# Raw weights loaded ahead of their split, the residual loaded by quarters with the first down operands on POOL's queue, and state-space units started by a table of steps

## The chip, the cores and the metric

The kernel runs on one core of a Trainium2 chip. The metric is the time of one execution on the device in microseconds (us), the median of several runs. One execution of each kernel is also profiled; all views of the trace are of that execution.

The engines, by the names the profile gives them: PE is TensorE (matrix products; its weight loads are PEld), DVE is VectorE, ACT is ScalarE, POOL is GpSimd, SP is SyncE, which in this kernel does nothing but start transfers. Each engine works through its own list of instructions in the order in which the program was laid out, and an instruction that waits holds up all that stand behind it on that engine.

## What is computed

One layer of a hybrid encoder over 2048 frames of 1024 features. A norm feeds one input projection. A quarter of its columns goes to a state-space layer (32 groups of 16 channels, each with 64 complex states), the rest to chunked attention (8 heads of 64, chunks of 64 frames, each looking at itself and the 8 chunks before). Both are normed and go through one output projection, then a SwiGLU block follows, both on the residual stream. Cut from the reference:

```python
h = rmsnorm(x, norm_mix_g)
proj = h @ w_in                       # u_ssm | q | k | v, 512 columns each
bu = einsum('bsgh,gph->bsgp', u, b_bar)
states = associative_scan(combine, (lam_bar, bu), axis=1)
y = einsum('bsgp,ghp->bsgh', states, c_mat).real + d_skip * u
y = gelu(y);  y = y * sigmoid(y @ w_glu + b_glu)
scores = einsum('bnqhd,bnkhd->bhnqk', qc, kb) / sqrt(64) + bias
out = einsum('bhnqk,bnkhd->bnqhd', softmax(masked scores), vb)
x = x + concat(rmsnorm(y), rmsnorm(out)) @ w_out
h2 = rmsnorm(x, norm_ffn_g)
x = x + (silu(h2 @ w_gate) * (h2 @ w_up)) @ w_down      # 2816 columns between
return rmsnorm(x, norm_final_g)
```

Everything is float32.

## The kernel before

**Numbers as two parts.** The matrix engine multiplies a shorter float format (`fp32r`), so each float32 operand is split in a high part, a cast on ScalarE, and a low part, a subtraction on VectorE (`split`, lines 153 to 156). A product is three matmuls, hi x hi, lo x hi and hi x lo (`mm3`, line 79). So before a matmul can start with a new weight tile its raw numbers must have landed, ACT must have cast them and DVE subtracted; rows with `hi`/`lo`, `w`, `c`, `hd` at line 156 are such splits.

**Stages, in us from the start of the span.** Until about 130: projection to the state-space input `u` and the first rows of attention. 130 to about 705: attention, into which the projections to q, k and v and the state-space units are woven. To 978: the state-space output's gate and the output projection. 980 to 1830: gate and up, as products of blocks with seven instead of eight block products (Strassen's way; B11, T1, T2, B22, T3, B21 and T4 name the seven). 1830 to the end: the down projection, again by seven, and the last norm.

**Attention.** There are 128 attention steps, four blocks of rows `sb` of 32 steps each, one step being one pair of heads of one group of chunks. A step computes scores `sc`, adds the bias (DVE, line 849), takes exponentials (ACT, line 852), transposes the probabilities `pt` (PE, line 82) and splits them into `pth` (ACT, line 867) and `ptl` (DVE, line 868). Between the steps stand pieces of *units*. A unit is a generator that yields after each piece; `Unit(gen, n, s0, s1, pre)` spreads its n pieces evenly over steps s0 to s1 - 1 and lets its first piece, the loads, run `pre` steps earlier. There are these units:

- `hT_unit`: loads and splits the 512 rows of the next block.
- `qk_unit(sb, pr)`: projects q and k of one pair of heads. Its first piece is `load_w` for two weight tiles. In block 0 these come from the input as `raw` tiles (line 689, two buffers) and are split into `w`; the split tiles are kept in memory as `wss` (`keep_w`, line 700) and later blocks load them from there (line 695). The matmuls into `pf` follow, then q and k are evacuated and split (`q2h`, `q2l`, `k`, lines 769 to 775).
- `v_unit(sb, fh)`: the same for v.
- `ssm_unit(b)`, for b = 0 to 7, four channel groups each. Loads of `U`, `Bst`, `Tm` and `Vm` (lines 564 on); after a pause of eight pieces the projection `X` in two pieces of two matmuls and four evacuations on ACT (line 588); then a scan over time on POOL alone (`step`, lines 602 to 605, and `carry`, lines 613 and 614), whose last states are moved into `XG` by four transfers that POOL starts (line 636); after nine more pieces the result `Y`, matmuls of `Tm` on `U` and `Vm` on `XG` (they go through `pj`), evacuation (line 646) and eight transfers to memory. `X` and `Y` use one buffer, and `U` has one buffer, so the loads of a unit wait for the `Y` of the one before.

Unit b of the state-space layer runs from step 2 + 15 b to 2 + 15 (b + 1); `SW = 15` sets that. In attention the order within a step is fixed by the program text, and a scheduler with estimated times may move instructions that are independent on the same engine.

**Down.** `down_phase` holds the output of the SwiGLU, already combined into the seven operands and stored as `hq`, and the weights, combined in advance, as `wc`. An `operand` (line 1487) loads 768 KB into a tile `hd` from a ring of ten tiles (line 1493, on SP) and splits it. `group(hf, f0, ...)` does the seven products for one half of the frames `hf` and three blocks of features from f0, and adds each to `acc` (line 1513). Each product is 36 matmuls (four banks of PSUM, three feature blocks, three matmuls each). In the first group of each half `load_acc` also loads the residual, eight tiles of 128 x 1024, 512 KB each (line 1518), right behind the first pair of operands in the text. Before its first product the last results `g` of gate and up have to be multiplied (DVE, line 1432) and stored (`hs<-g`, line 1434, on SP).

Of the kernel before, what the change touches and what calls it, by code (L numbers as in the profile page):

```python
# [49 lines left out]
SW = 15  # L50
# [46 lines left out]
def f32(ap):  # L97
    return ap.bitcast(F32)
# [557 lines left out]
class Unit:  # L656


    def __init__(self, gen, n, s0, s1, pre=0, done=0, light=1):
        self.gen, self.n, self.s0, self.s1, self.pre, self.done = gen, n, s0, s1, pre, done  # L660
        self.room = lambda a, b: sum(light if s % 4 == LPH else 1 for s in range(a, b))

    def advance(self, s):

        if s < self.s0 - self.pre:
            return
        want = 1
        if s >= self.s0:
            want += math.ceil((self.n - 1) * self.room(self.s0, s + 1) / self.room(self.s0, self.s1) - 1e-9)
        if s >= self.s1 - 1:  # L670
            want = self.n + 1
        while self.done < want:
            self.done += 1
            if next(self.gen, self) is self:
                self.done = 1 << 30


def att_phase(k, ident, S, aw, x0, roots):

    tc, nc, io, pfs = k.tc, k.nc, k.io, k.pfs  # L680
    with ExitStack() as cx:
        hT, vts, qk, keep = {0: tuple(zip(*x0))}, {}, {}, {}

        def load_w(sb, n):

            w = k.t(aw, "w", [P, 2, 1024], F32R, bufs=WB)
            if sb == 0:
                raw = k.t(aw, "raw", [P, 1024], bufs=2)
                nc.sync.dma_start(raw[:], io["w_qk"][n] if n < 8 else io["w_v"][n - 8])
                for ins in split(k, w[:, 0], w[:, 1], raw[:]):  # L690
                    if n in (0, 4):
                        k.tc.keep_in_program_order(ins)
                keep[n] = w
            else:
                nc.sync.dma_start(f32(w[:]), S["ws"][n])
            return w[:, 0], w[:, 1]
# [35 lines left out]
        def qk_unit(sb, pr):  # L732
            ws = [load_w(sb, n) for n in (pr, 4 + pr)]
# [48 lines left out]
        def v_unit(sb, fh):  # L782
            ws = [load_w(sb, 8 + 2 * r + fh) for r in range(2)]
# [143 lines left out]
        for sb in range(NSB):  # L927
            g0 = sb * 32
            C = CUT if sb < NSB - 1 else CUTL
            if sb > 0:  # L930
                if DB:
# [3 lines left out]
            units += [ Unit(qk_unit(sb, 1), QK_N, g0 + C[2], g0 + C[3], 2, light=LIGHT),  # L935
                      Unit(qk_unit(sb, 2), QK_N, g0 + C[3], g0 + C[4], 2, light=LIGHT), Unit(v_unit(sb, 1), V_N, g0 + C[4], g0 + C[5], 2, light=LIGHT),
                      Unit(qk_unit(sb, 3), QK_N, g0 + C[5], g0 + C[6], 2, light=LIGHT)]
        for b in range(NG // GB):
            units.append(Unit(ssm_unit(k, sp, psum, S, b, k.ssm_eng), SSM_N, 2 + int(SW * b), 2 + int(SW * (b + 1)), light=SL))
# [535 lines left out]
def down_phase(k, S):  # L1475
    tc, nc, io = k.tc, k.nc, k.io
    V, te = nc.vector, k.te
    with ExitStack() as cx:
# [8 lines left out]
        def operand(src, early=False):  # L1487
# [4 lines left out]
            with tc.high_priority() if early else ExitStack():  # L1492
                nc.sync.dma_start(f32(lo), src.rearrange("g p c -> p g c"))
# [3 lines left out]
        def group(hf, f0, g, acc, early):  # L1497

            fs = slice(f0, f0 + g)
            x, y = [bank(dx) for _ in range(4)], None  # L1500
            for n, on_x, first, r, c in ((B11, 1, 1, 0, 0), (T1, 0, 1, 1, 1), (T2, 1, 0, 0, 1), (B22, 0, 0, 0, 1), (T3, 1, 0, 1, 1), (B21, 0, 1, 0, 0), (T4, 1, 0, 1, 0)):
# [13 lines left out]
        def load_acc(hf, acc):  # L1515
            for i in range(KT):
                a = k.t((a0, a1)[hf], f"acc{i}", [P, HALF])
                nc.sync.dma_start(a[:], S["x1"][i * P : (i + 1) * P, hf * HALF : (hf + 1) * HALF])
                acc.append(a)
# [177 lines left out]
```

## Time and profile before

| | us |
|---|---|
| three runs | 2287.0, 2295.97, 2296.15; median 2295.97 |
| profiled execution | 2289.1 |
| its span, first to last instruction | 2287.1 |
| busy in the span: PE / DVE / ACT / POOL | 2171.6 / 1544.7 / 1000.6 / 348.7 |
| mean granted clock of TensorE | 0.978 of full |
| moved by transfers | 428.33 MB, of it 412.50 MB from hardware queues and 13.91 MB from the software queue, where POOL's transfers go |

The span is what lies between the first and the last instruction; 2.0 us of the execution lie around it. A row of the timeline has a start, a duration, the engine, the line, the operation, out<-in and shape, how many, and in brackets the idle time of that engine before it and what ended it. A group of waits has the total, the number and the longest. "SPq" rows are issues on SP; their duration includes the time the queue was held. The granted clock (PEclk) is the share of full speed that TensorE's throttle allowed.

### The profile page before, as it was taken

To read this page: it belongs to the slowest core of one execution; us is meant where nothing else is said; L and a number is where in the kernel's file an instruction comes from. 1 tells how busy PE (TensorE), PEld (TensorE's weight loads), DVE (VectorE), ACT (ScalarE), POOL (GpSimd) and SP (SyncE) were. 2 spreads that over 40 slices of the span, in tenths; PEclk is the share of its full clock that TensorE was granted. 3 is DMA by queue.
4 is the path that set the end of the run, shared out by engine and by line. 5 is a ranking of instruction groups with operands and counts; after the bars stand their busy time and mean duration, and the time that the engine had idled before them with its cause. 6 is when DMAs were issued, how large, how long until landed. Compare 5 with 4: busy or idle time off the path is not lost.

```text
span 2287.1 us, 30278 instructions
## 1 busy us (share of the span) xinstructions
PE 2171.6 (95%) x10632; PEld 1830.1 (80%) x10632; DVE 1544.7 (68%) x2695; ACT 1000.6 (44%) x1654; POOL 348.7 (15%) x813
## 2 busy tenths in 40 slices
PE   8988899999996899999999999999999989999997
PEld 6777688898985788878888887888888778888886
DVE  7755565555556766876776678666666477789776
ACT  6444555455557652343333335333333343344322
POOL 2245765455660000000000000000000000000000
PEclk9998999999998999999999999999999999999999
DMA  8767886666644534854465567555423297465552
GB/s 299 236 221 220 257 223 201 187 188 179 188 132 124 171 121 147 267 189 151 160 200 178 167 211 258 203 169 188 139 96 110 78 341 252 166 212 193 206 189 74
DMA packets 215256, 428.33 MB, mean 187 GB/s; under 512 B 38592, under 2 KB 61168, under 8 KB 208000
## 3 DMA queue, kind: packets, MB, share of 16 engines
q1 hardware_dynamic: 210368, 412.50, 55.3%
q0 software_dynamic: 4736, 13.91, 2.0%
q8 instruction: 83, 1.36, 0.2%
q14 instruction: 69, 0.57, 0.1%
HBM read 286.86 MB, written 129.00 MB: 182 GB/s over the span
## 4 chain that ended last, share of the span: by engine, by line
PE 80%; DVE 6%; DMA 4%; POOL 4%; issue 3%; ACT 1%; SPq 1%; DVEq 0%; POOLq 0%; ACTq 0%
PE X L79 20%; PE ps L79 19%; PE Y L79 10%; PE pf L79 9%; PE big L79 9%; PE W L79 5%; PE pj L79 4%; PE sc L79 2%; PE pt L82 2%; DMA xt<-in_xp 1%; DMA hd<-wc 1%; POOL X L605 1%; DVE lo L156 1%; POOL X L604 1%; POOL st L602 1%
## 5 line engine op out<-in xcount | busy, mean ns | idle before, releaser
L79 PE MATMUL X<-hi,c 128*128 128x512 f32 x1408 | 451.0, 391 | 6.9 <-DVE c L156 5.4
L79 PE MATMUL ps<-hd,hd 128*128 128x512 f32 (+1 forms) x1968 | 430.8, 381 | 6.1 <-ACT hd L156 4.5
L79 PEld LDWEIGHTS ps<-hd,hd 128*128 128x128 f32 x1968 | 358.0, 189 | 77.7 <-ACT hd L156 5.3
L79 PEld LDWEIGHTS X<-hi,c 128*128 128x128 f32 x1408 | 265.3, 189 | 63.4 <-DVE c L156 6.3
L79 PE MATMUL X<-lo,c 128*128 128x512 f32 x704 | 274.9, 391 | 0.0
L156 ACT CAST hd<-hd 128x1536 fp32r<-128x1536 f32 (+1 forms) x106 | 147.7, 1393 | 236.3 <-DMA hd<-hq 178.7
L79 PE MATMUL Y<-hi,c 128*128 128x512 f32 x704 | 224.7, 390 | 1.5 <-DVE u L1389 1.5
L156 DVE TENSOR_TENSOR hd<-hd 128x1536 fp32r<-128x1536 f32 (+1 forms) x106 | 174.4, 1646 | 29.1 <-ACT hd L156 28.4
L156 DVE TENSOR_TENSOR c<-S,c 128x512 fp32r<-128x512 f32 x176 | 121.0, 689 | 98.3 <-ACT c L156 98.0
L1385 ACT COPY u<-X 128x512 f32<-128x512 f32 x132 | 77.4, 587 | 200.7 <-PE X L79 200.7
L1513 DVE TENSOR_TENSOR acc<-acc,ps 128x512 f32<-128x512 f32 x196 | 130.9, 684 | 50.3 <-PE ps L79 47.8
L156 ACT CAST c<-S 128x512 fp32r<-128x512 f32 x176 | 109.4, 622 | 120.1 <-PE Y L79 61.6
L79 PE MATMUL pf<-hi,w 128*128 128x512 f32 x416 | 153.9, 422 | 8.4 <-ACT w L156 4.7
L79 PE MATMUL big<-m,woh 128*128 128x512 f32 x512 | 161.2, 396 | 0.0
L79 PEld LDWEIGHTS Y<-hi,c 128*128 128x128 f32 x704 | 132.5, 188 | 29.9 <-DVE u L1389 2.2
L79 PEld LDWEIGHTS X<-lo,c 128*128 128x128 f32 x704 | 132.8, 189 | 27.5
L156 ACT CAST c<-raw 128x512 fp32r<-128x512 f32 x132 | 82.3, 623 | 150.5 <-PE Y L79 68.5
L79 PE MATMUL Y<-lo,c 128*128 128x512 f32 x352 | 137.2, 390 | 0.0
L868 DVE TENSOR_TENSOR ptl<-pt,pth 128x640 fp32r<-128x640 f32 (+3 forms) x152 | 98.3, 647 | 47.5 <-ACT pth L867 45.9
L852 ACT ACTIVATE s<-s,mn 128x640 f32<-128x640 f32 (+4 forms) x128 | 98.0, 765 | 65.6 <-DVE mn L849 61.1
L867 ACT CAST pth<-pt 128x640 fp32r<-128x640 f32 (+3 forms) x152 | 83.8, 551 | 95.6 <-PE pt L82 91.5
L79 PE MATMUL W<-hi,c 128*128 128x512 f32 x352 | 115.5, 389 | 0.0
(441 smaller groups left out, 4169.9 us busy)
## 6 DMA issues: line engine op xcount, KB each, us to landing
w<-wss SPq DMA_DIRECT2D x36, 1024.0 KB, 6.0
hq<-g SPq DMA_DIRECT2D x140, 256.0 KB, 2.1
hd<-hq SPq DMA_DIRECT2D x42, 768.0 KB, 4.5
hd<-wc SPq DMA_DIRECT2D x42, 768.0 KB, 6.0
raw<-in_w_gate SPq DMA_DIRECT2D x44, 512.0 KB, 3.8
raw<-in_w_up SPq DMA_DIRECT2D x44, 512.0 KB, 4.3
wc<-px SPq DMA_DIRECT2D x66, 256.0 KB, 3.2
wss<-w SPq DMA_DIRECT2D x12, 1024.0 KB, 5.7
```

Source lines behind the costliest of these rows:

```text
L79: return self.tc.keep_in_program_order(self.tc.nc.tensor.matmul(*a, **b))
L82: return self.tc.keep_in_program_order(self.tc.nc.tensor.transpose(*a, **b))
L156: return nc.scalar.copy(hi, raw), nc.vector.tensor_tensor(lo, raw, f32(hi), op=ALU.subtract)
L602: eng.tensor_tensor(t[:, :, :, :n], src, ar, op=ALU.mult)
L604: eng.tensor_tensor(dst, dst, t[:, :, :, :n], op=ALU.add)
L605: eng.tensor_tensor(dst, dst, t2[:, :, :, :n], op=ALU.add)
L852: nc.scalar.activation(s[:, :nk], s[:, :nk], AF.Exp, bias=mn[:], scale=-1.0, accum_out=sums[sb, pr][:, hh, qp : qp + 1])
L867: nc.scalar.copy(pth[:, a:b, qp, :], pt[:, a:b, :])
L868: nc.vector.tensor_tensor(ptl[:, a:b, qp, :], pt[:, a:b, :], f32(pth[:, a:b, qp, :]), op=ALU.subtract)
L1385: nc.scalar.copy(u[:], ps[:])
L1513: V.tensor_tensor(a, a, ps[:], op=ALU.add)
```

## The change

Three things are edited.

1. `load_w` becomes `load_raw` and `load_ws`. In block 0 both raw tiles of a unit are loaded first, then, after a `yield`, both are split. The units of block 0 for qk(0,1), qk(0,2), v(0,1) and qk(0,3) get one piece more, `pre = 4` (the loads four steps ahead) and a new argument `mid = 2` (the second piece, the split, two steps ahead); both were two steps ahead. The first unit and v(0,0) keep load and split together. Later blocks load from `wss` as before.
2. `SW = 15` becomes the table `SU`: the eight state-space units start at steps 2, 19, 35, 49, 64, 78, 93 and 107 and the last ends at 122, instead of 2, 17, 32, 47, 62, 77, 92, 107 and 122.
3. In the down phase, in the first group of each half, the operands of a product are loaded in the text one product ahead; in the very first group (`early`) all fourteen operands are issued from POOL's queue (`aside`); and the residual is loaded in quarters, 128 x 512, 256 KB, four at a time in the order in which the products add to them.

```diff
-SW = 15
+SU = 2, 19, 35, 49, 64, 78, 93, 107, 122
@@ class Unit
-        want = 1
+        want = 1 if self.mid is None or s < self.s0 - self.mid else 2
         if s >= self.s0:
-            want += math.ceil((self.n - 1) * self.room(self.s0, s + 1) / self.room(self.s0, self.s1) - 1e-9)
+            want += math.ceil((self.n - want) * self.room(self.s0, s + 1) / self.room(self.s0, self.s1) - 1e-9)
@@ attention
-        def load_w(sb, n):
...
+        def load_raw(n):
+            raw = k.t(aw, "raw", [P, 1024], bufs=2)
+            nc.sync.dma_start(raw[:], io["w_qk"][n] if n < 8 else io["w_v"][n - 8])
+            return raw
+
+        def load_ws(sb, ns):
+            raws = [load_raw(n) for n in ns] if sb == 0 else []
+            if raws and ns not in ((0, 4), (8, 10)):
+                yield
+            ws = []
+            for i, n in enumerate(ns):
+                w = k.t(aw, "w", [P, 2, 1024], F32R, bufs=WB)
+                if raws:
+                    for ins in split(k, w[:, 0], w[:, 1], raws[i][:]):
+                        if n in (0, 4):
+                            k.tc.keep_in_program_order(ins)
+                    keep[n] = w
+                else:
+                    nc.sync.dma_start(f32(w[:]), S["ws"][n])
+                ws.append((w[:, 0], w[:, 1]))
+            return ws
...
-            ws = [load_w(sb, n) for n in (pr, 4 + pr)]
+            ws = yield from load_ws(sb, (pr, 4 + pr))
...
+            for gen, n, c in ((qk_unit(sb, 1), QK_N, 2), (qk_unit(sb, 2), QK_N, 3), (v_unit(sb, 1), V_N, 4), (qk_unit(sb, 3), QK_N, 5)):
+                units.append(Unit(gen, n, g0 + C[c], g0 + C[c + 1], 2, light=LIGHT) if sb else Unit(gen, n + 1, C[c], C[c + 1], 4, light=LIGHT, mid=2))
-            units.append(Unit(ssm_unit(k, sp, psum, S, b, k.ssm_eng), SSM_N, 2 + int(SW * b), 2 + int(SW * (b + 1)), light=SL))
+            units.append(Unit(ssm_unit(k, sp, psum, S, b, k.ssm_eng), SSM_N, SU[b], SU[b + 1], light=SL))
@@ down_phase
-                nc.sync.dma_start(f32(lo), src.rearrange("g p c -> p g c"))
+                (nc.gpsimd if aside else nc.sync).dma_start(f32(lo), src.rearrange("g p c -> p g c"))
...
-                h = operand(S["hq"][hf, fs, n], early and n in (B11, T1))
-                w = operand(S["wc"][fs, n], early and n in (B11, T1))
-                if n == B11 and f0 == 0:
-                    load_acc(hf, acc)
+            def load(m):
+                if m < len(order):
+                    n = order[m][0]
+                    soon = early and n in (B11, T1)
+                    ops[n] = operand(S["hq"][hf, fs, n], soon, early), operand(S["wc"][fs, n], soon, early)
+
+            if f0 == 0:
+                acc += [k.t((a0, a1)[hf], f"acc{i}", [P, HALF]) for i in range(KT)]
+                load(0)
+            seen = set()
+            for m, (n, on_x, first, r, c) in enumerate(order):
+                load(m + 1 if f0 == 0 else m)
+                if f0 == 0 and (r, c) not in seen:
+                    seen.add((r, c))
+                    load_acc(hf, acc, r, c)
+                h, w = ops.pop(n)
...
-        def load_acc(hf, acc):
-            for i in range(KT):
-                a = k.t((a0, a1)[hf], f"acc{i}", [P, HALF])
-                nc.sync.dma_start(a[:], S["x1"][i * P : (i + 1) * P, hf * HALF : (hf + 1) * HALF])
-                acc.append(a)
+        def load_acc(hf, acc, r, c):
+            for i in range(4 * r, 4 * r + 4):
+                cs = slice(hf * HALF + c * 512, hf * HALF + (c + 1) * 512)
+                nc.sync.dma_start(acc[i][:, c * 512 : (c + 1) * 512], S["x1"][i * P : (i + 1) * P, cs])
```

What this does to the order of instructions at three places, all in lists of one engine. Lines of the changed kernel are 8 to 21 higher than those of the kernel before.

VectorE about step 7 of attention, before. `w_1859` and `w_1864` are the weights of qk(0,2); `k_349` and `k_352` the keys of the pair of heads before; `ptl` and `yt` belong to the attention steps and to the evacuation of q and k.

```order
L892 TENSOR_TENSOR ya_1890<-pj_1891,yt_1900 64x512
L868 TENSOR_TENSOR ptl_1904<-pt_1905,pth_1903 128x128
L762 TENSOR_TENSOR yt_1915<-pf_1808,rsn_92 128x512
L849 ISA s_1944,mn_1945<-sc_1941,nbb_1549 128x512
L868 TENSOR_TENSOR ptl_1904<-pt_1948,pth_1903 128x128
L775 TENSOR_TENSOR k_349_1690<-yt_1915,k_349_1690 64x512
L775 TENSOR_TENSOR k_352_1693<-yt_1915,k_352_1693 64x512
L878 RECIPROCAL rs_2090<-sm_1566 128x8
L868 TENSOR_TENSOR ptl_1904<-pt_1948,pth_1903 128x128
L156 TENSOR_TENSOR w_1859<-raw_1860,w_1859 128x1024
L156 TENSOR_TENSOR w_1864<-raw_1865,w_1864 128x1024
```

And after, where the same weights are called `w_1856` and `w_1859` and the keys again `k_349` and `k_352`:

```order
L156 TENSOR_TENSOR w_1856<-raw_1780,w_1856 128x1024
L900 TENSOR_TENSOR ya_1884<-pj_1885,yt_1894 64x512
L156 TENSOR_TENSOR w_1859<-raw_1782,w_1859 128x1024
L876 TENSOR_TENSOR ptl_1898<-pt_1899,pth_1897 128x128
L770 TENSOR_TENSOR yt_1909<-pf_1812,rsn_92 128x512
L857 ISA s_1938,mn_1939<-sc_1935,nbb_1549 128x512
L857 ISA mn_1939 128x1
L876 TENSOR_TENSOR ptl_1898<-pt_1942,pth_1897 128x128
L783 TENSOR_TENSOR k_349_1690<-yt_1909,k_349_1690 64x512
L783 TENSOR_TENSOR k_352_1693<-yt_1909,k_352_1693 64x512
```

The two subtractions moved from behind the keys to ahead of them.

TensorE at the projection of state-space unit 0, whose two pieces are the matmuls into `pj_1816` and `pj_1823` (before):

```order
L79 MATMUL pf_1808<-hi_188_991,w_1607 128x512
L79 MATMUL pj_1816<-U_1705,Bst_1714 128x256 x2
L79 MATMUL pj_1823<-U_1705,Bst_1714 128x256 x2
L79 MATMUL sc_1830<-lo2x_1388,hi1x_1386 128x256
L79 MATMUL sc_1830<-lo2x_1388,lo1x_1387 128x256
L82 MATMUL pt_1837<-ident_79,s_1730 128x128 x4
```

And after, where they are `pj_1820` and `pj_1862`:

```order
L79 MATMUL pf_1812<-hi_188_991,w_1609 128x512
L79 MATMUL pj_1820<-U_1705,Bst_1714 128x256 x2
L79 MATMUL sc_1827<-lo2x_1388,hi1x_1386 128x256
L79 MATMUL sc_1827<-lo2x_1388,lo1x_1387 128x256
L82 MATMUL pt_1834<-ident_79,s_1730 128x128 x4
...
L79 MATMUL pf_1812<-hi_196_999,w_1609 128x512
L79 MATMUL pj_1862<-U_1705,Bst_1714 128x256 x2
```

The second piece of the projection moved behind the scores, the transposes and twelve matmuls of the q and k projection (18 rows in all); its evacuation on ACT splits four and four in the same way.

SP at the start of the down phase, before: four operands of B11 and T1, eight residual tiles, then the operands of T2.

```order
L1493 DMA hd_17187<-wc_76 128x3x512
...
L1518 DMA acc_3157_17127<-x_5_67 128x1024
L1518 DMA acc_3158_17129<-x_5_67 128x1024
...
L1518 DMA acc_3164_17141<-x_5_67 128x1024
L1493 DMA hd_17235<-hq_75 128x3x512
L1493 DMA hd_17239<-wc_76 128x3x512
```

After, the last rows of POOL's list are the fourteen operands (B11, T1, T2 and so on); SP's list has the residual of both halves instead:

```order
L1500 DMA hd_17127<-hq_75 128x3x512
L1500 DMA hd_17131<-wc_76 128x3x512
L1500 DMA hd_17135<-hq_75 128x3x512
L1500 DMA hd_17139<-wc_76 128x3x512
L1500 DMA hd_17187<-hq_75 128x3x512
L1500 DMA hd_17191<-wc_76 128x3x512
L1500 DMA hd_17243<-hq_75 128x3x512
```

```order
L1441 DMA hs_73<-g_16992 128x512
L1539 DMA acc_3156_17120<-x_5_67 128x512
...
L1539 DMA acc_3162_17126<-x_5_67 128x512
L1539 DMA acc_3283_18497<-x_5_67 128x512
L1539 DMA acc_3284_18498<-x_5_67 128x512
```

Sixteen quarters of the first half are followed on SP by the sixteen of the second (`acc_3283` and on), ahead of the operands of the second group. The order of TensorE's matmuls in the down phase is unchanged.

More of the change, by code (lines that the diff above doesn't have):

```diff
@@ L782, in v_unit @@
         def v_unit(sb, fh):
-            ws = [load_w(sb, 8 + 2 * r + fh) for r in range(2)]
+            ws = yield from load_ws(sb, (8 + fh, 10 + fh))
             yield
@@ L1499, in group @@
             fs = slice(f0, f0 + g)
+            order = (B11, 1, 1, 0, 0), (T1, 0, 1, 1, 1), (T2, 1, 0, 0, 1), (B22, 0, 0, 0, 1), (T3, 1, 0, 1, 1), (B21, 0, 1, 0, 0), (T4, 1, 0, 1, 0)
             x, y = [bank(dx) for _ in range(4)], None
[L1501 to L1505 removed]
+            ops = {}
+            def load(m):
[13 more added lines that the diff above has]
+                h, w = ops.pop(n)
                 if not on_x and first:
```

20 lines of the change are left out of this document (3 added, 17 removed).

## The prediction

> **What bounds the kernel now.** I read the page first. The chain of work that ended last is by four fifths matmuls of TensorE:
>
> ```profile
> PE 80%; DVE 6%; DMA 4%; POOL 4%; issue 3%; ACT 1%; SPq 1%; DVEq 0%; POOLq 0%; ACTq 0%
> ```
>
> The change takes no matmul away, so it can win only idle time of TensorE and the slow clock behind such idle time. Its idle time by cause is in the view of waits (total, times, longest); these groups the change can touch:
>
> ```profile
> PE pj L79 <- DMA Tm<-kts: 11.1, 4, 3.7
> PE pf L79 <- ACT w L156: 4.7, 1, 4.7
> PE ps L79 <- ACT hd L156: 4.5, 2, 2.7
> PE pj L79 <- DMA XG<-X: 3.6, 2, 1.9
> ```
>
> Together 23.9 us, 1% of the span. The timeline of TensorE shows where they stand (start, duration, instruction, then the idle time ahead of it and who ended it):
>
> ```profile
> 167.90 0.44 PE L82 MATMUL pt<-ident,s 128*128 128x128 f32 x2
> 173.01 0.79 PE L79 MATMUL pf<-hi,w 128*128 128x512 f32 x1 [4.67 <-ACT w L156]
> 177.42 0.31 PE L79 MATMUL sc<-k,q2h 128*128 128x128 f32 x1
> 193.50 0.87 PE L82 MATMUL pt<-ident,s 128*128 128x128 f32 x3 [3.36 <-DVE ptl L868]
> 212.53 0.67 PE L79 MATMUL pj<-XG,Vm 128*128 128x256 f32 x2 [1.68 <-DMA XG<-X]
> 281.66 0.67 PE L79 MATMUL pj<-XG,Vm 128*128 128x256 f32 x2 [1.94 <-DMA XG<-X]
> 300.02 1.35 PE L79 MATMUL pj<-U,Bst 128*128 128x256 f32 x5 [2.92 <-DMA Tm<-kts]
> 364.46 1.75 PE L79 MATMUL pj<-U,Bst 128*128 128x256 f32 x7 [3.00 <-DMA Tm<-kts]
> 1831.46 0.73 PE L79 MATMUL ps<-hd,hd 128*128 128x512 f32 x2 [1.78 <-ACT hd L156]
> 1833.25 16.16 PE L79 MATMUL ps<-hd,hd 128*128 128x512 f32 x70 [1.06 <-DVE hd L156]
> 1852.12 1.22 PE L79 MATMUL ps<-hd,hd 128*128 128x512 f32 x2 [2.70 <-ACT hd L156]
> ```
>
> A stall can cost more than its length. In two-microsecond windows (busy times, then the granted clock, the DMA share and GB/s):
>
> ```profile
> core 0: us, PE busy (x) PEld busy (x) DVE busy (x) ACT busy (x) POOL busy (x), PEclk, DMA share, GB/s
> 172.00:174.00 2.00, 0.99 (x2) 0.50 (x2) 1.01 (x1) 1.91 (x3) 1.92 (x4) 0.53 0.34 130
> 174.00:176.00 2.00, 1.96 (x5) 1.44 (x5) 1.67 (x2) 0.00 (x0) 1.92 (x2) 0.50 0.51 217
> 176.00:178.00 2.00, 2.00 (x8) 1.61 (x8) 0.02 (x1) 0.00 (x0) 1.84 (x5) 0.50 0.96 329
> 194.00:196.00 2.00, 2.00 (x7) 1.61 (x6) 0.72 (x2) 0.64 (x2) 1.69 (x5) 0.50 0.96 397
> 300.00:302.00 2.00, 1.98 (x10) 1.78 (x11) 0.00 (x0) 0.79 (x3) 0.00 (x0) 1.00 0.35 70
> 1854.00:1856.00 2.00, 2.00 (x5) 1.61 (x6) 1.76 (x1) 1.53 (x2) 0.00 (x0) 0.50 1.05 410
> ```
>
> After 4.67, 3.36 and 2.70 us of idling the clock stands at 0.50, after 2.92 at 1.00. Six microseconds at half clock do three of work: half of 0.99, 1.96 and 2.00 is 2.5 us from 172 to 178, so I charge 2.5 to 3 us for each such stall. The Trainium skill (TensorE: Matmul & The Clock Gate, HAM oscillation) says that idle gaps above about 3.4 us bring the slow clock; the 2.70 us gap shows that here a shorter one can, and by that rule the down phase would have 2.8 us less to win than I count.
>
> **Raw weights earlier.** Four units of the first 512 rows get their raw weights four steps ahead and split them two steps ahead. The first wait this meets is the one at 173.01. Around it stand on VectorE:
>
> ```profile
> 169.29 1.84 DVE L775 TENSOR_TENSOR k<-yt,k 64x512 fp32r<-64x512 f32 x2
> 172.99 2.68 DVE L156 TENSOR_TENSOR w<-raw,w 128x1024 fp32r<-128x1024 f32 x2 [1.47 <-ACT w L156]
> 188.77 1.23 DVE L156 TENSOR_TENSOR w<-raw,w 128x1024 fp32r<-128x1024 f32 x1
> 193.08 0.28 DVE L868 TENSOR_TENSOR ptl<-pt,pth 128x128 fp32r<-128x128 f32 x1
> ```
>
> The instructions are the same; two casts on ScalarE and two subtractions on VectorE (2.68 us) move ahead of the split of k. So k is late next: without the weights' wait TensorE would have nine matmuls (2.0 us at 16.16/70 = 0.23 each) from 168.35 to the scores now at 177.42, thus come at 170.4, but the k split, ending at 171.13 now, gets 2.68 us of VectorE ahead of it. Wholly exposed that makes 173.8, wholly in idle time 171.1; I take the middle, 172.4. Gain at that place 177.42 - 172.4 = 5.0, and 0.9 more as the half clock's rest behind it goes: 5.9 (4.5 to 7.2). At 193.50 the released row is `ptl` behind a second subtraction; the new order puts it ahead of that one and of a `ya` row, so some 2.0 of the 3.36 go, and with them the half clock: up to 5 more. The DMAs moved are two raw loads of 512 KB, on SP ahead of four q loads that nobody waits for in these views; I cost them at nothing.
>
> **Unit spacing.** But what stands next on the path is unit 0's scan. It runs so:
>
> ```profile
> 159.68 3.02 ACT L588 COPY X<-pj 64x256 f32<-64x256 f32 x8 [0.24 <-PE pj L79]
> 162.85 0.51 POOL L602 TENSOR_TENSOR st<-X,a 128x128 f32<-128x128 f32 x1 [24.00 <-ACT X L588]
> 205.53 1.21 POOL L636 DMA_DIRECT2D XG<-X x2 [0.30 <-POOL X L614]
> 304.31 0.50 POOL L602 TENSOR_TENSOR st<-X,a 128x128 f32<-128x128 f32 x1 [28.50 <-ACT X L588]
> 344.63 1.21 POOL L636 DMA_DIRECT2D XG<-X x2 [0.30 <-POOL X L614]
> DMA to landing us min/median/max: 2.4/4.6/7.9
> ```
>
> From eight evacuations to the last XG issued POOL takes 162.85 to 206.74, and TensorE waits for its landing until 212.53. In the new order the second half of unit 0's projection comes 18 matmuls (3.4 us) later and its evacuation is split four and four; half of the 3.02 us now overlaps, so the scan starts about 2 us later and XG lands at about 214.5. Against that, Y of unit 0 gets 5.7 us more work ahead of it (matmuls counted in the order, at 0.23 us for 512 columns). The old kernel has that work done at 212.5 + 5.7 = 218, so all that was won before is cut to 218 - 214.5 = 3.5. The wait for XG itself grows: 10.9 us won less these 3.5, plus the old 1.68, is 9 us, and a wait so long should bring half clock, 3 us again. Through unit 0: 0.5 won (bounds -2 if the scan starts the full 3.4 us later, 10.9 if it keeps up).
>
> The later units need three rows more, SP's issues (start, duration) and the first matmul of unit 2's Y:
>
> ```profile
> 285.58 3.61 SPq L649 DMA_DIRECT2D y<-X  x8
> 291.59 3.53 SPq L564 DMA_DIRECT2D U<-u  x7
> 348.70 0.59 PE L79 MATMUL pj<-U,Tm 128*128 128x256 f32 x2
> ```
>
> Unit 1 has 2.9 us more work between its projection and Y, so the 1.94 at 281.66 goes (+1.9). Unit 2's loads of U no longer stand behind a weight load on SP, which waited for its buffer and kept them from 289.19 to 291.59, 2.4 us; work before it is 0.5 less: +1.9 of the 2.92. Unit 3 gets 3.4 us more work between unit 2's Y and its own projection: the 3.00 go (+3.0). In exchange units 2 and 4 have 5.6 and 6.2 us less work under their scans. Unit 2's last XG is issued at 345.84, so with the shortest landing, 2.4, it is there 48.2 us after the projection began at 300.02. Y came at 348.70, 48.7 us after it, without a wait; with 5.6 less work it comes at 43.1: a new wait of up to 5.6 if the scan takes as long as now, 0 if it shrinks along. I take 4, near the upper end since the scan's instructions are unchanged, and 2 for half clock behind it (two chances in three of 3). For unit 4 I take 1.0 (0 to 2.2). Sum of the attention part: 0.5 + 1.9 + 1.9 + 3.0 - 6.0 - 1.0 = 0.3 won; from -7 to +15.
>
> **The down phase.** The rows that carry it (SP's rows are issues; the window's last columns are granted clock, DMA share, GB/s):
>
> ```profile
> 1831.56 5.88 SPq L1518 DMA_DIRECT2D acc<-x  x8
> 1837.58 0.44 SPq L1493 DMA_DIRECT2D hd<-hq  x1
> 1848.70 1.47 ACT L156 CAST hd<-hd 128x1536 fp32r<-128x1536 f32 x1 [12.84 <-DMA hd<-hq]
> 1842.00:1853.00 11.00, 8.30 (x35) 6.32 (x33) 5.91 (x7) 3.37 (x3) 0.00 (x0) 0.93 1.04 410
> ```
>
> Now eight residual loads (4.2 MB, 5.88 us of issue) stand ahead of T2's operands, which are issued at 1837.58, cast only at 1848.70, and TensorE waits 2.70 us for them at 1852.12. With the operands on POOL, idle by then, T2's pair goes out six microseconds sooner. This should take the 2.70 and the half clock behind it, 2.8: 5.5 won, nothing lost beside it while the queue delivers. Each POOL issue is charged 0.6 (1.21 for two, the XG row), off the path. The first wait, 1.78 and 1.06, I leave: the subtraction of the first weights still stands behind the last `g` product on VectorE; POOL's issue may be up to 1 us earlier or later. The extra sixteen small residual issues cost SP about another 5.9 us per half in a stretch where nothing that TensorE needs stands behind them until the second group, some 55 us on. I count the 5.5 in full; the bounds are -13 (rival 2 below) and 6.5 (the first wait a little shorter too).
>
> Sum: 0.3 + 5.5 = 5.8 us. The profiled execution took 2289.1 (span 2287.1 and 2.0 around it), which gives 2283.3. The three runs are 2287.0, 2295.97 and 2296.15, so their median stands 6.9 above the profiled one and would give 2290. I write 2283, the sum on the execution that it is made from.
>
> **Rivals.** (1) *The scan keeps up.* POOL's forty-four microseconds in unit 0 were partly slowed beside VectorE's subtractions; unit 2 takes 41.5 for the same work. If the moved splits no longer collide, XG comes two or three microseconds sooner, and if no wait exceeds the length that drops the clock, unit 0 keeps 6 to 7 instead of 0.5 and units 2 and 4 lose nothing: 5.8 + 6 + 7 = 18.8, or 2270. For it: the difference 43.9 against 41.5. Against: the order puts unit 0's second half later.
>
> (2) *Contention in the down phase, slower than before.* The new order puts all residual, 8.4 MB of both halves, on SP at once beside the operands on POOL; before, the second half came with the second group. From 1842 to 1853 the engines already run at a share of 1.04 and 410 GB/s. Residual and the pairs of T2, B22 and T3 (4.7 MB) are 13.1 MB, 32 us at 410 GB/s, where T3 is wanted within about 31 us of 1831 (16.16 us for two products, two more to come, less the splits). If POOL's queue gets half, a pair of 1.57 MB takes 7.7 us, less than a product's 8.2: no wait. If it gets a third, a pair takes 11.5 us, and three products wait 3.3 each with half clock behind them, 18.3 us against the 5.5 removed: with 0.3 from the attention part 2289.1 + 18.3 - 5.5 - 0.3 = 2302. It decides from a share of 0.47 down. The Trainium skill (DMA: Bandwidth & Descriptors, Queues, rings and completion order) says that each engine takes turns between the queues it has work for, packet by packet; by it the share would be about half, which is just on the good side. No run here shows both queues loaded.
>
> (3) *Units 2 and 4 wait at full price.* For it: their scans are the ones whose cover shrinks. Against: XG's landing has been as short as 2.4. Waits of 5.6 and 2.2 with 3 us of half clock after each cost 13.8 where I count 7: 2283.3 + 6.8 = 2290, no change.
>
> (4) *The down part does nothing:* POOL's T2 issue waits for buffers that TensorE and ScalarE still hold, so it goes out hardly before 1837. Then only 0.3 is won, 2289.
>
> **How the numbers follow.** The bound for faster and slower is 0.5%, 11.5 us, about what a measurement of this kernel tells from no change. Forecast 0.43, (1) 0.22, (2) 0.14, (3) 0.12, (4) 0.09. The forecast's own range is 2276 to 2291; it splits into 0.20 faster and 0.23 same, since it stands 5.8 below the profiled execution and 13 below the median. (1) is all faster. (2) gives 0.12 slower and 0.02 same, (3) 0.11 same and 0.01 slower, (4) 0.08 same and 0.01 slower. Sums: faster 0.42, same 0.44, slower 0.14. The range runs from just below rival 1 to rival 2, 2268 to 2302.
>
> **What would show it.** Right: no wait for `w` near 170; a wait for `XG` at unit 0 above 5 us with half clock; none at unit 1's; no `U` wait for units 2 and 3; in the down phase no gap before T2 and a clock of 1.00 from 1850 on. Wrong: the first XG wait under 3 us (rival 1), waits for `hd` after `DMA` at B22 or T3 (rival 2), or POOL's T2 issue later than 1836 (rival 4). The forecast fails as a whole if the state-space stage ends earlier or later than its waits account for, or if a new wait appears in gate and up, which the change leaves alone.

## The result and the profile after

| | before | after |
|---|---|---|
| median of 20 runs each, us | 2295.59 (2282.42 to 2302.85) | 2292.34 (2285.17 to 2300.38) |
| profiled execution, us | 2289.1 | 2293.41 |
| ratio | | 0.9992, 95% interval 0.9978 to 1.0005 |

No change that can be told. The forecast was 2283, 0.25% below the profiled execution of before. That the profiled execution got longer while the median got shorter lies within the spread of single runs, 20 us before and 15 us after; the verdict is the ratio, the trace tells where time moved.

The view of waits of the changed kernel, whole span, answers to the four groups of the prediction:

```profile
PE pj L79 <- DMA XG<-X: 14.2, 2, 8.4
PE pt L82 <- DVE ptl L876: 13.5, 11, 3.2
PE pj L79 <- DMA Tm<-kts: 8.1, 5, 3.8
PE ps L79 <- DVE hd L156: 2.0, 2, 1.8
PE ps L79 <- DVE acc L1534: 1.2, 1, 1.2
```

The wait for `w` is gone, that for `hd` went from 4.5 and 1.6 to 2.0, and that for `XG` grew from 3.6 to 14.2. TensorE's timeline of the changed kernel has the places:

```profile
171.23 0.44 PE L82 MATMUL pt<-ident,s 128*128 128x128 f32 x2 [3.20 <-DVE ptl L876]
218.44 1.19 PE L79 MATMUL pj<-XG,Vm 128*128 128x256 f32 x2 [8.45 <-DMA XG<-X]
235.53 1.10 PE L79 MATMUL pj<-U,Bst 128*128 128x256 f32 x4 [1.88 <-DMA Tm<-kts]
312.32 0.89 PE L79 MATMUL pj<-U,Bst 128*128 128x256 f32 x3 [0.66 <-DMA Tm<-kts]
376.40 0.89 PE L79 MATMUL pj<-U,Bst 128*128 128x256 f32 x3 [0.22 <-DMA Tm<-kts]
450.35 0.89 PE L79 MATMUL pj<-U,Bst 128*128 128x256 f32 x3 [1.59 <-DMA Tm<-kts]
499.64 0.77 PE L79 MATMUL pj<-XG,Vm 128*128 128x256 f32 x1 [5.79 <-DMA XG<-X]
633.02 0.68 PE L79 MATMUL pj<-XG,Vm 128*128 128x256 f32 x2 [1.95 <-issue]
722.16 0.79 PE L79 MATMUL pf<-gh,wgh 128*128 128x512 f32 x1 [6.81 <-ACT gh L156]
1842.33 57.00 PE L79 MATMUL ps<-hd,hd 128*128 128x512 f32 x250 [1.76 <-DVE hd L156]
1900.52 0.70 PE L79 MATMUL ps<-hd,hd 128*128 128x512 f32 x2 [1.19 <-DVE acc L1534]
```

The first matmul of the gate after attention, here at 722.16, stood in the kernel before at:

```profile
714.56 0.79 PE L79 MATMUL pf<-gh,wgh 128*128 128x512 f32 x1 [6.76 <-ACT gh L156]
```

So attention ends 7.6 us later. Since the matmuls other than the state-space ones come in the same order in both kernels, each can be set against its twin (times of the kernel before): the changed kernel is 6.8 us ahead at 207 us, 2.7 behind at 222 (after unit 0's Y), 0.1 behind at 485, 8.2 behind at 497 (after unit 4's Y), 4.8 behind ahead of unit 6's Y and 8.6 after it, 7.6 at the gate. By 1820 it is 9.9 behind (gate and up add 2.3, which is in no part that the change touches), by 1862 2.7, by 1903 4.2. The down phase gives 5.8 back; attention had lost more than that.

Two waits for XG are followed by the slow clock. Windows of the changed kernel (busy times, granted clock, DMA share, GB/s):

```profile
218.00:220.00 2.00, 1.56 (x4) 1.33 (x5) 0.00 (x0) 0.00 (x0) 0.00 (x0) 0.50 0.00 0
220.00:222.00 2.00, 2.00 (x7) 1.56 (x6) 0.00 (x0) 0.58 (x2) 0.00 (x0) 0.50 0.00 0
500.00:502.00 2.00, 2.00 (x6) 1.56 (x6) 0.00 (x0) 0.00 (x0) 0.00 (x0) 0.50 0.05 10
```

What unit 0 waited for stands on POOL:

```profile
166.18 0.53 POOL L602 TENSOR_TENSOR st<-X,a 128x128 f32<-128x128 f32 x1 [27.21 <-ACT X L588]
211.60 1.21 POOL L636 DMA_DIRECT2D XG<-X  x2 [0.30 <-POOL X L614]
492.15 1.21 POOL L636 DMA_DIRECT2D XG<-X  x2 [0.30 <-POOL X L614]
```

The scan starts 3.3 us later than before (166.18 against 162.85) and takes 46.6 instead of 43.9 us. In unit 4 the last issue starts at 492.8 and XG has landed at 500.1, 7.4 us later; in the kernel before the same unit's XG had landed 4.6 us after its issue, and Y came behind it. (All landing times here are counted from the start of the issue.) What XG met on its way were loads of the split weights, 1 MB each, on SP's queue:

```profile
209.73 0.72 SPq L702 DMA_DIRECT2D w<-wss  x1
490.17 0.33 SPq L702 DMA_DIRECT2D w<-wss  x1
560.07 0.32 SPq L702 DMA_DIRECT2D w<-wss  x1
624.94 0.33 SPq L702 DMA_DIRECT2D w<-wss  x1
```

The last two XG of units 0, 4, 5 and 6 were issued 0.1 to 2.6 us behind these and landed after 6.2 to 7.8 us. Unit 1's, beside loads of `xt`, took 7.2 and 7.8. Those of units 2, 3 and 7, with no large load beside them, landed after 2.4 to 5.0. The three units whose Y waits for XG (0, 4 and 6) are all among those with a weight load; units 1 and 5 had work enough ahead of their Y.

### The profile page after: what moved, and what is told of

It is laid out like the page before. It is cut to its first block, busy times and chain, and to the rows that moved or that the text cites. A ratio compares the mean times of both kernels' runs of the same rounds, so it can differ in the third digit from the quotient of the medians.

```text
span 2291.6 us, 30320 instructions
## 1 busy us (share of the span) xinstructions
PE 2172.1 (95%) x10632; PEld 1828.7 (80%) x10632; DVE 1542.1 (67%) x2695; ACT 1000.9 (44%) x1654; POOL 359.2 (16%) x827
## 4 chain that ended last, share of the span: by engine, by line
PE 73%; POOL 8%; issue 6%; DVE 4%; DMA 3%; ACT 2%; SPq 1%; DVEq 0%; POOLq 0%; ACTq 0%
PE X L79 20%; PE ps L79 17%; PE Y L79 10%; PE big L79 9%; PE pf L79 5%; PE W L79 5%; PE pj L79 3%; POOL X L605 2%; POOL st L602 1%; POOL st L603 1%; POOL X L604 1%; POOL X L614 1%; POOL fx L613 1%; PE sc L79 1%; PE pt L82 1%
## 5 line engine op out<-in xcount | busy, mean ns | idle before, releaser
L1500 POOL DMA_DIRECT2D hd<-hq x7 | 5.3, 764 | 1133.4 <-PE X L79 1121.1
L860 ACT ACTIVATE s<-s,mn 128x640 f32<-128x640 f32 (+4 forms) x128 | 98.0, 765 | 58.5 <-DVE mn L857 53.6
```

The lines of the kernel that those rows point to most:

```text
L860: nc.scalar.activation(s[:, :nk], s[:, :nk], AF.Exp, bias=mn[:], scale=-1.0, accum_out=sums[sb, pr][:, hh, qp : qp + 1])
```

## The experiments

Attention runs from the first score matmul to the first gate matmul. "Idle" adds up the gaps of TensorE above 0.2 us in it, in brackets those ahead of state-space matmuls; "slow clock" adds up what the clock record falls short of full speed. These three are from one profiled execution each, which can lie several us off the median. Before, e3, e7 and e11 have the same program text in attention and spread from 577.2 to 582.2, so 5 us in that column are no effect by themselves. The ratio is over several runs, in brackets its 95% interval.

| kernel | ratio to before | attention | idle | slow clock |
|---|---|---|---|---|
| before | | 582.2 | 57.5 (14.7) | 31.7 |
| the change | 0.9992 (0.9978 to 1.0005) | 589.6 | 64.0 (24.3) | 32.0 |
| e1 raw weights alone | 1.0013 (0.9998 to 1.0028) | 578.1 | 57.3 (16.6) | 27.9 |
| e2 spacing alone | 1.0015 (1.0 to 1.003) | 587.5 | 57.4 (19.3) | 34.3 |
| e3 down alone | 0.9968 (0.9956 to 0.9981) | 580.0 | 55.4 (12.4) | 31.8 |
| e4 without spacing | 0.998 (0.9966 to 0.9994) | 581.0 | 60.4 (18.1) | 25.8 |
| e5 raw, short scan | 1.0006 (0.9985 to 1.0027) | 578.6 | 57.9 (14.8) | 28.2 |
| e6 unit 4 longer | 1.0001 (0.9981 to 1.0021) | 589.9 | 66.1 (25.7) | 30.3 |
| e7 down, all on SP | 0.9974 (0.9957 to 0.999) | 577.2 | 56.5 (14.9) | 25.7 |
| e8 cover table | 0.9915 (0.989 to 0.994) | 566.1 | 47.5 (11.4) | 21.9 |
| e9 cover, no raw | 0.9915 (0.9887 to 0.9942) | 573.5 | 52.0 (13.1) | 25.7 |
| e10 cover, no pieces | 0.9947 (0.9929 to 0.9965) | 582.0 | 58.5 (19.3) | 29.9 |
| e11 down, whole residual | 0.9996 (0.9979 to 1.0013) | 578.6 | 57.1 (13.7) | 26.5 |
| e12 cover alone | 0.9961 (0.9939 to 0.9982) | 578.7 | 51.9 (15.3) | 31.6 |
| e13 cover, raw, down on SP | 0.9901 (0.9879 to 0.9924) | 564.6 | 45.0 (9.5) | 24.6 |
| e14 cover, no raw, down on SP | 0.9938 (0.992 to 0.9955) | 568.5 | 52.5 (12.8) | 19.7 |

**The three parts, one at a time and two together.** e1 to e3 are the kernel before with that part's hunks of the diff; e4 is the changed kernel with

```diff
-SU = 2, 19, 35, 49, 64, 78, 93, 107, 122
+SU = 2, 17, 32, 47, 62, 77, 92, 107, 122
```

> The kernel before with the raw weights ahead alone (spacing and down phase as before). Theory A (unit 0's scan on POOL is the bound behind the weights' wait): no wait for w at 173, TensorE comes to unit 0's Y some 10 us earlier and waits there for XG 8 to 12 us instead of 1.68, with half clock behind it; at 230 us it stands within 3 us of before, end of attention within 3 us, time ratio 0.999 to 1.002. Rival B (the moved splits themselves slow ScalarE, VectorE and POOL): later by 4 us or more at unit 0's Y, ratio above 1.002. Rival C (the gain is kept): ratio below 0.997.

> The kernel before with the table of steps alone. Theory A: the w wait of 4.67 stays; unit 0's XG wait near 0 to 4 (the scan starts 2 to 3 us later, 5.7 us more work ahead of Y); units 2 and 3 lose their load waits; units 4 and 6 wait for XG 4 to 6 and 1 to 2 us with half clock, as with the whole change; end of attention 2 to 8 us later than before, ratio 1.001 to 1.004. Rival B: spacing alone is harmless or a gain, ratio at or below 1.000.

> The kernel before with the changed down phase alone. All theories take it for the part that gains: attention as before, the T2 gap of 2.70 gone, 5 to 6 us gained from the first down product to the end, ratio 0.9970 to 0.9982. If it gains under 2 us, the gain seen in the whole change's profile came from the later start and not from the edit.

> The changed kernel with units every 15 steps again (raw weights ahead and down phase as changed). Theory A: attention as in the raw-alone run, down gain 5 to 6, together 3 to 7 us faster than before, ratio 0.997 to 0.9985, so better than the whole change by 2 to 6 us. Rival B: attention later than before by 4 us or more, ratio 0.999 to 1.001, no better than the whole change.

e4 came out within theory A's range, though its interval overlaps that of the whole change. The ratios add up: 1.0013, 1.0015 and 0.9968 make 0.9996, measured 0.9992. The down phase gains 0.3%, clearly; the two parts in attention give about as much back, each by itself not clear of nothing. In e1 the wait for `w` is gone and unit 0's Y is reached 8 us sooner, at 202 instead of 210, where TensorE stands until XG lands:

```profile
209.23 0.77 PE L79 MATMUL pj<-XG,Vm 128*128 128x256 f32 x1 [6.44 <-DMA XG<-X]
```

It goes on 3.3 us ahead of the 212.53 of before, and half clock and the next units' loads leave 1 us of that at 224. That is theory A, with a wait below what it said (6.44 against 8 to 12). It missed the end of attention, 4.0 us earlier than before where it had said within 3; the profile is of the fastest of e1's twelve runs, and the ratio shows no gain. In e2 the wait for `w` stays, so unit 0's Y does not wait at all, and units 1, 4 and 6 do, unit 4 with 4.55; the sign is what theory A said, the size near its lower end.

**Is it the scan?** e5 is e1 with

```diff
-    yield from carry(Xk[:, :, :, 1:, :7], Xk[:, :, :, : NC // 8 - 1, 7], 0, NC // 8 - 1)
+    if b:
+        yield from carry(Xk[:, :, :, 1:, :7], Xk[:, :, :, : NC // 8 - 1, 7], 0, NC // 8 - 1)
+    else:
+        yield
+        yield
```

> The kernel before with the raw weights ahead alone, and the last, longest carry of unit 0's scan (four pairs of POOL instructions of 128x434) left out, so that unit 0's state is not the reference's. Theory A (unit 0's scan is what swallowed the gain): XG of unit 0 lands about 8 us sooner than in the raw-alone run, the 6.44 us wait falls below 1, TensorE stands 6 to 8 us ahead of the kernel before at 223 us, and keeps 4 to 8 of it to the end unless unit 1's or 2's loads and scan take it again; ratio 0.996 to 0.999. Rival (the time is lost anyway, to the later units' loads and scans, which are spaced as before): the gain at 223 is there but under 2 us is left at 350 us; ratio 1.000 or above.

The ratio is the rival's, the reason neither's: the scan ends 9.5 us sooner and the wait hardly moves, 5.08 instead of 6.44. The timelines of e5 on POOL, SP and PE show it:

```profile
197.14 1.21 POOL L640 DMA_DIRECT2D XG<-X  x2 [0.30 <-POOL X L614]
...
193.88 1.06 SPq L712 DMA_DIRECT2D wss<-w  x2
194.99 2.61 SPq L690 DMA_DIRECT2D raw<-in_w_qk  x2
...
208.79 0.77 PE L79 MATMUL pj<-XG,Vm 128*128 128x256 f32 x1 [5.08 <-DMA nbb<-nbs]
```

The row of TensorE names `nbb`; of the four XG the third landed at 208.52, just ahead of it. The last XG is issued at 197.8 and has landed at 209.7, 12.0 us later; in e1 it took 2.5. Ahead of it in time SP had issued two kept weight tiles of 1 MB and two raw tiles of 512 KB, and the engines were full:

```profile
198.00:202.00 4.00, 3.62 (x30) 3.39 (x29) 2.26 (x9) 2.73 (x10) 0.35 (x1) 1.00 1.10 256
```

So right behind the scan stands a second bound at the same time, 209 us. That it is this traffic which holds XG up is argued from the rows; a run without it was not made. For it: the same two raw loads, issued at 194.01 and 195.18 in e1, where the first XG went out only at 200.95, landed there after 7.9 and 8.0 us, and here, beside all four XG, after 12.7 and 14.0. What follows is that a shorter scan alone isn't the cure; e8 tries more work ahead of Y.

**Which unit's cover.** e6 is the change with `SU = 2, 19, 35, 49, 64, 79, 93, 107, 122` (79 for 78).

> The changed kernel with one number of the table moved: unit 4 ends and unit 5 starts at step 79 instead of 78. Theory A (unit 4's cover decides): unit 4 gets 5.5 us more work under its scan, its XG wait of 5.79 falls below 1.5 without half clock, unit 5 has 3.6 us less and still does not wait more than 1; attention ends 6 to 10 us sooner than in the whole change, ratio to before 0.995 to 0.9975. Rival (XG lands late there because of what else is moved at that time): the wait stays above 3, ratio 0.9985 or above.

Its wait for XG at unit 4 is gone, as theory A said, but the time is not: unit 5, whose step was taken, waits for its loads and then for XG (and unit 0's wait came out 1.0 longer, 9.45).

```profile
515.43 1.19 PE L79 MATMUL pj<-U,Bst 128*128 128x256 f32 x2 [2.51 <-DMA Tm<-kts]
...
566.86 0.67 PE L79 MATMUL pj<-XG,Vm 128*128 128x256 f32 x2 [1.88 <-issue]
```

Theory A held for the mechanism and failed in the sum: one number can't be moved alone, since units share a fixed number of steps. e8 therefore sets all of them by the matmuls that stand under each scan (38 to 48 us), and gives unit 0 more without parting its projection; e10 is e8 without the pieces:

```diff
-SU = 2, 19, 35, 49, 64, 78, 93, 107, 122
+SU = 2, 19, 34, 49, 63, 78, 92, 107, 122
@@ ssm_unit
-    for _ in range(YX):
+    for _ in range(YX + 5 * (b == 0)):
@@ units
-            units.append(Unit(ssm_unit(k, sp, psum, S, b, k.ssm_eng), SSM_N, SU[b], SU[b + 1], light=SL))
+            units.append(Unit(ssm_unit(k, sp, psum, S, b, k.ssm_eng), SSM_N + 5 * (b == 0), SU[b], SU[b + 1], light=SL))
```

> The changed kernel with another table (2, 19, 34, 49, 63, 78, 92, 107, 122) and five more empty pieces ahead of unit 0's Y alone, so that unit 0's projection is not parted and its Y has 39 us of work ahead of it instead of 34, and each later unit 38 to 48. Theory A (cover under each scan decides): unit 0's XG wait falls from 6 to 8 us to 0 to 3, no other XG wait above 2; with the down gain of 7 attention gains 2 to 7, ratio 0.994 to 0.9965, the best of the kernels so far. Rival (the gain is eaten by load waits of the next units): ratio 0.9965 to 0.9985.

> The changed kernel with that table alone, without the five empty pieces, so that unit 0's projection is parted in two again and its Y has 36 us of work ahead instead of 39. Theory A (unit 0's scan starts too late for its Y): unit 0's XG wait is back at 6 to 9 us with half clock, attention 8 to 11 us longer than with the pieces, ratio 0.995 to 0.9965. Rival (the later units' spacing is what gained, and a late unit 0 is made up by them): ratio 0.991 to 0.9935.

e8 is 0.85% faster than before, more than expected, and unit 0's Y hardly waits. What is left is unit 5:

```profile
211.55 0.67 PE L79 MATMUL pj<-XG,Vm 128*128 128x256 f32 x2 [0.47 <-DMA XG<-X]
...
544.76 1.19 PE L79 MATMUL pj<-XG,Vm 128*128 128x256 f32 x2 [3.19 <-issue]
```

Without the five pieces (e10), the same row reads:

```profile
218.88 1.19 PE L79 MATMUL pj<-XG,Vm 128*128 128x256 f32 x2 [8.98 <-DMA XG<-X]
```

That is 8.5 us more of wait and, by ratios taken on different chips, 7 us of time (0.9947 against 0.9915; the intervals overlap a little). The parting of unit 0's projection, a by-product of the wider spacing, is the start of it and not the whole: TensorE comes 1.2 us earlier to this Y, the last two XG are issued 1.9 us later, and the first of them lands after 8.6 instead of 3.2 us. In e8 they go out ahead of the next 1 MB weight load, in e10 with it (e8's two rows first, then e10's):

```profile
208.12 1.21 POOL L636 DMA_DIRECT2D XG<-X  x2 [0.30 <-POOL X L614]
210.68 0.32 SPq L702 DMA_DIRECT2D w<-wss  x1
210.05 1.21 POOL L636 DMA_DIRECT2D XG<-X  x2 [0.30 <-POOL X L614]
210.09 0.55 SPq L702 DMA_DIRECT2D w<-wss  x1
```

Unit 5 shows the same without an edit: e8 and e13 (below) have the same program text in attention. In e8 the first of its last two XG is issued 0.1 us behind such a load, they land after 7.1 and 8.3 us, and Y waits 3.19. In e13 the first of them is issued 1.5 us ahead of it, and they land after 3.4 and 4.1, and Y, which came 1.4 us later there counted from the projection, does not wait. e12 against e9 and e14, again with one attention text, is the same: 6.7 and 8.0 us behind the load, 2.8 to 3.1 ahead of it. Over all the traces, 38 of the 40 last XG that were issued with such a load or up to 2.7 us behind it landed after 6.2 to 8.9 us (the two others, of unit 1 in e1 and e4, after 3.4 and 2.6). No run moved the weight loads alone.

**Are the weights worth moving?** e9 is e8 without the hunks of the raw weights. e12 is the kernel before with e8's table and pieces alone. e13 and e14 are e8 and e9 with all down operands on SP, on one chip.

> The table of the best kernel so far (2, 19, 34, 49, 63, 78, 92, 107, 122, five empty pieces ahead of unit 0's Y) and the changed down phase, but the weights loaded and split as before the change. Theory A (moving the raw weights pays once unit 0's Y has cover): the w wait of 4.7 with half clock is back and nothing makes it up, attention 4 to 9 us longer than with the weights ahead (566 us there), ratio 0.993 to 0.9955. Rival (the table alone does it, the weights ahead are worth nothing): attention within 3 us of 566, ratio below 0.9925.

> The kernel before with the other table (2, 19, 34, 49, 63, 78, 92, 107, 122) and the five empty pieces ahead of unit 0's Y, nothing else. Theory A (the spacing's effect has the sign of the cover that it leaves under each scan): attention 5 to 10 us shorter than before, ratio 0.9945 to 0.9975, where the change's own table alone gave 1.0015. Rival (any spacing other than 15 steps only pays together with the changed down phase or the weights): ratio 0.999 or above.

> That table and pieces, the raw weights ahead and the changed down phase with its operands on SP's queue. Theory A (the weights ahead pay once unit 0's Y has cover): 3 to 7 us less than the run without them in this call, ratio 0.990 to 0.993. Rival (worth nothing): within 2 us of it.

> The same without the raw weights ahead. Theory A: 3 to 7 us more than the run with them in this call, ratio 0.992 to 0.995, attention 4 to 9 us longer. Rival: within 2 us of it, attention within 3 us.

e9 against e8, measured on different chips, fits the rival by the ratio (0.9915 both) and theory A by the profile (7 us, but of the slowest of e9's six runs). On one chip e13 and e14 have medians of 2268.76 and 2278.25, 9.5 us apart, more than theory A's 3 to 7; their intervals just touch, and in the profiles attention is 3.9 us longer, just short of the 4 to 9 expected. The profiled execution of e14, 2271.24, is the fastest of its six. In it the old wait stands:

```profile
171.33 0.80 PE L79 MATMUL pf<-hi,w 128*128 128x512 f32 x1 [4.67 <-ACT w L156]
```

So the weights ahead are worth nothing without cover (e1), and probably something with it: 9.5 us by the medians of the one pair on one chip, nothing by the ratios of the other pair. How much stays open. e12 shows the sign of the spacing turn with e8's table and pieces alone: 0.9961, where the change's own table gave 1.0015 (attention is 3.5 us shorter in its profile, less than theory A said and within the spread of one program). e13, at 0.9901, has the lowest ratio of the versions tried and is faster than both kernels; e8's interval overlaps its own.

**The down phase.** e7 is e3 with all operands on SP; e11 is e7 with the residual whole again:

```diff
-                (nc.gpsimd if aside else nc.sync).dma_start(f32(lo), src.rearrange("g p c -> p g c"))
+                nc.sync.dma_start(f32(lo), src.rearrange("g p c -> p g c"))
@@ e11 also (its load_acc with whole tiles is not shown)
...
-                if f0 == 0 and (r, c) not in seen:
-                    seen.add((r, c))
-                    load_acc(hf, acc, r, c)
+                if f0 == 0 and m == 0:
+                    load_acc(hf, acc)
```

> The kernel before with the changed down phase alone, but all operands on SP's queue: one product ahead and residual by quarters are kept, POOL's queue is not used. Theory A (POOL's queue is what gets T2's operands out ahead of the residual): a wait for hd of 2 us or more with half clock at T2 or B22 is back, ratio 0.999 to 1.001. Rival (order of loads and quarters do it alone): no such wait, ratio as with POOL's queue, 0.996 to 0.998.

> The kernel before with the changed down phase on SP's queue, but the residual in eight whole tiles of 512 KB, all of them ahead of T2's operands again. Theory A (the order of the residual against T2's operands is what gained, and quarters are what allows it): a wait for hd of 2 to 4 us with half clock at T2 is back, ratio 0.999 to 1.001. Rival (it is the loads one product ahead): no such wait, ratio 0.9965 to 0.998.

The rival wins in e7: without POOL's queue the gain is the same (0.9974 against 0.9968). After the first two waits the row of e7 runs through 126 matmuls without a gap:

```profile
1828.10 0.73 PE L79 MATMUL ps<-hd,hd 128*128 128x512 f32 x2 [2.25 <-ACT hd L156]
1829.89 30.45 PE L79 MATMUL ps<-hd,hd 128*128 128x512 f32 x126 [1.06 <-DVE hd L156]
```

With the residual whole, and the operands still one product ahead in the text, T2's gap is back and the gain gone (0.9996), as theory A said:

```profile
1827.64 16.17 PE L79 MATMUL ps<-hd,hd 128*128 128x512 f32 x70 [1.12 <-DVE hd L156]
1846.89 1.01 PE L79 MATMUL ps<-hd,hd 128*128 128x512 f32 x2 [3.08 <-ACT hd L156]
```

It is the quarters that allow the order: with them one MB of residual instead of four stands ahead of T2's operands. Quarters without the loads one product ahead were not run, and the intervals of e7 and e11 overlap, so that the gap at T2 carries this reading.

## Why the prediction failed, step by step

The step that failed is the sum for attention, 0.3 won: it mis-sized the waits for XG at units 0 and 4 and left out the one at unit 6. The runs showed 7.6 us lost there in the profile. At units 4 and 6 XG landed late, behind weight loads that the sum did not count; at unit 0 the scan started later and took longer than summed.

- **What bounds it:** right. No matmul went, and time moved with waits and with the slow clock behind them.
- **Raw weights:** the wait for `w` went; what came late next was not k but `ptl` (3.20 at 171.23), which the two subtractions also stand ahead of. The wait at 193.50 did shrink, to 1.49 (at 188.32). TensorE was 6.8 us ahead before unit 0's Y, where 10.9 had been summed up.
- **Unit 0's scan:** the mechanism was right and said ahead: a wait of 9, measured 8.45, with half clock. Mis-sized was XG's landing, 214.5 against 218.4: the scan started 3.3 instead of 2 us later and took 2.7 us longer. The longer scan goes with the moved splits: it took 45.3 to 46.6 us in the seven kernels that have them (e5 aside) and 43.9 to 44.6 in the eight that do not. Instead of 0.5 won, 2.7 were lost through unit 0.
- **Waits of units 1 to 3:** about right. Unit 1's 1.94 for XG went; the load waits of 2.92 and 3.00 became 0.66 and 0.22. A new one of 1.59 came at unit 4.
- **Units 2, 4 and 6, the step that failed most.** Unit 2 was given a wait of 4 and has none: its scan took 38.1 instead of 40.9 us from the first `st` to the start of the last XG issue, and TensorE needed 4.1 us more for the work under it, 2.4 of idling and 1.7 of half clock, which the prediction had not counted, so that the missing wait was in part luck. (The sum there also adds 2.4 to the end of the last issue, 345.84, while the view counts landings from its start, 345.25; that XG landed at 348.73.) Unit 4 was given 1.0 and cost 8 with its half clock. Its bound of 2.2 comes out with XG's landing at 2.4, the shortest in the profile; here the last two landed after 7.4 us, behind the 1 MB weight load issued at 490.17. In the kernel before that load was issued at 490.02, when XG had landed (487.89). Unit 6's wait (1.95, and 3.9 with the clock) was not seen at all; its last two XG landed after 7.4 and 7.8 us, behind the load issued at 624.94. So the sum for attention was 0.3 won and came out as 7.6 lost in the profile; by the runs e1 and e2 it is 0.28% lost, 6 us, each half within a few us of nothing.
- **Down:** 5.5 forecast, 5.8 in the profile and 0.32% (7 us) in e3: the size was right and the cause half right. It was put down to POOL's queue; POOL's first T2 issue waited for a split (1838.96, against 1839.45 for the first product), and e7 shows that the queue is not needed. A small new wait, 1.19 at 1900.52 for `acc` additions that had fallen behind on VectorE, was not foreseen.

```profile
1838.96 0.76 POOL L1500 DMA_DIRECT2D hd<-hq  x1 [9.37 <-ACT hd L156]
```

- **Rivals:** (1) did not come, the scan took longer and not shorter. (3), the waits of units 2 and 4 at full price with 2290 and no change, is the nearest in time, though it was unit 4 and 6 and not 2. (2) did not come: with residual on SP and operands on POOL TensorE met no wait for `hd` at B22 or T3 (the row from 1842.33 runs through 250 matmuls). After one that landed at 1846.25, six more operands of 768 KB from POOL's queue had landed by 1863.74, which is 270 GB/s, where windows from 1842 to 1862 show 411 to 419 GB/s in all. By this estimate its share was 0.65, above the 0.47 that decides. The Trainium skill's rule that the queues take turns (DMA: Bandwidth & Descriptors, Queues, rings and completion order) had been read as about half; the trace gives POOL's queue more. (4) was half true: POOL's issue did wait, until after the 1836 that was named as the sign, but the whole phase came later. Counted from the first product, T2's first operand went out 6.6 us sooner than before, and the wait did no harm. The Trainium skill's bound of about 3.4 us of idling before the slow clock (TensorE: Matmul & The Clock Gate, HAM oscillation) fits the 5.79 and 8.45 of the changed kernel and is too long for the 2.70 and 3.36 of the kernel before.

## What to carry to other kernels

When a wait is removed in front of a second one, the time goes to the second: ask first what TensorE meets next and whether that thing gets earlier too. Where one engine works under another's cover, spread the work by the matmuls that stand under each stretch, all stretches at once, and check that a wider spacing does not part the piece that starts the hidden work. A transfer that lies on the path should be costed with the long end of its landing times wherever other large transfers are due: here XG landed after 3 to 4 us where it went out a microsecond or two ahead of a 1 MB load, and, with two exceptions, after 6 to 9 where it went out with it or just behind.

## What was not expected

- The landing of a 127.5 KB XG transfer took from 2.3 to 12.0 us, and with POOL done 9.5 us sooner it landed at the same time (209.7 against 209.8).
- Splitting 4 MB of residual into quarters in order of need, with the operands loaded one product ahead, gained 0.3% without another queue.
